# Where a recurrence's output products stand among the attention's scores, and which engine does one of the last additions

## The chip, the cores and the metric

The kernel runs on one core of one Trainium2 chip. The core has a matrix engine (TensorE, PE in the profile), a vector engine (VectorE, DVE), a scalar engine (ScalarE, ACT), a general engine (GpSimd, POOL) and SyncE (SP), which here only issues transfers. Each engine runs its own instructions in order, and they wait for one another by semaphores. The metric is the device time of one execution in microseconds (us). Of the kernel before the change three runs were timed: 451.43, 451.46 and 453.24 us, median 451.46. One further execution was profiled; all rows below are from it.

## The reference

One decoder layer on 512 tokens with 1024 features, in float32. Cut to what matters here:

```python
xn = rmsnorm(h)
aq, ak, av, ag, bq, bf, bi, bg, gate_a, gate_b = split(xn @ w_in)
ya = moba_attention(norm(aq), norm(ak), av)          # 8 heads x 64, relative-position bias
ya = (ya * silu(ag)) @ w_up_a
yb = hgrn2_chunkwise(silu(bq), kb, bi, log_f)        # 4 heads, state 128 x 128
yb = (rmsnorm(yb) * silu(bg)) @ w_up_b
merged = sigmoid(gate_a) * ya + sigmoid(gate_b) * yb
h = h + merged @ w_out
return h + (p @ w_ple) * sigmoid(h @ w_ple_gate)
```

Inside the recurrence, each chunk's output is `scores @ v + (q * exp(cum)) @ state`.

## The kernel before, in words

A large product is computed as three products of rounded halves (high x high, low x high, high x low; `mm3`, line 289), each weight and each operand being split into two float32r tiles by ScalarE (the high half) and VectorE (the rest). A projection of the 1024 features is 24 such products of 128 x 128 by 128 x 512. TensorE's order is written out by hand. A planner walks through the projections in the list `ORDER` and keeps a clock of its own (`now`): after every three products it adds their time and runs the side streams that are due (`tick`, `run_due`). A side stream is a generator that issues a piece of work and then names a delay or a condition for its next piece. The engines other than TensorE are not written out: a scheduler orders their instructions from dependences, priorities and a timing model, so that a small move on TensorE can turn over the order of VectorE, ScalarE and SP around it.

Two side streams matter.

The attention (`attention`, line 788) takes the eight heads as four head pairs (0 to 3) and each pair in two runs (`STEPS`): the first run has the query blocks 0, 1 and 2, the second has query block 3. A run issues its `scores` products (line 815), then `softmax`: VectorE subtracts from the bias and takes the row minimum (line 832), ScalarE takes the exponential and scales (834, 836), VectorE turns 32 x 32 blocks (839); then sixteen small transfers on SP's queue finish the transpose (line 850). The values follow at the end of a pair (`out_values`, line 863, tiles o0 to o3), behind the first scores of the next pair. `PACE` is the planner's delay between the runs: 19.5 behind a first run and 22.5 behind a second. Each pair needs two rows of bias, 256 KB each, which `bias` (line 880) loads on SP's queue into a pool of three buffers, 8 planner microseconds ahead of the pair's first run.

The recurrence (`hgrn_intra`, `hgrn_out`) goes through its four heads. For head h it prepares decayed keys and queries (the hx tiles), waits until an attention run has been issued (`beside_attention`, line 501), and computes small products for the scores inside a chunk (lpb, lpa: lines 592 to 649). `hgrn_out` computes the states (line 663, tiles hds and st). Its output products (tile hop, lines 678 and 680) are, for heads 0 to 2, not issued but put on the list `hops`; `hgrn_intra` of the next head takes them from there (line 583) behind its `beside_attention`, that is right behind the scores of an attention run, and ahead of its own lpb products. The output products add 1.5 to the planner's clock. The fourth head issues its own, without the list. Behind them ScalarE squares (692), VectorE applies gain and gate (695) and a norm follows (313 to 334, 698).

At the end of the kernel the last product is made in half sums for pairs of 128 output features. `merge` (line 1181) then takes the sigmoid, multiplies by the embedding's product (line 1189, VectorE), adds the residual (line 1190: VectorE for n = 3 and n = 7, otherwise GpSimd) and stores (line 1191, SP). The last pieces are output block n = 3: its right half, then columns 0 to 127 (product tile pe3l) and last columns 128 to 255 (pe3m).

Of the kernel before, what the change touches and what calls it, by code (L numbers as in the profile page):

```python
# [15 lines left out]
OP = mybir.AluOpType  # L16
# [12 lines left out]
LEVELS = (16, 8, 4, 2, 1)  # L29

STEPS = ((0, 1, 2), (3,))
PACE = (19.5, 22.5)

HP = 2.5
H0 = 8.0
# [33 lines left out]
def hybrid_layer_kernel(  # L69
# [17 lines left out]
    V, A, G, PE = nc.vector, nc.scalar, nc.gpsimd, nc.tensor  # L87
# [14 lines left out]
    def bank(tag, name):  # L102
        return psum.tile([128, 512], F32, tag=tag, bufs={"mm": 3, "g": 2, "a": 3}[tag], name=name)
# [34 lines left out]
    def cost(us):  # L138
        now[0] += us
# [18 lines left out]
    def held_from(us, insts, until=None):  # L158

        def later():  # L160
            for inst in insts if until not in done else []:
                held(inst)
            yield 0.0

        spawn(later(), us)
# [331 lines left out]
    hops = []  # L497
# [290 lines left out]
    def attention(qn, kn, va, sags, res):  # L788
        def place(qb, j):

            return {0: (j, 0), 1: (2, 256 * j), 2: (j, 128), 3: (j, 0)}[qb]

        def tiles(step):
            return 2 + (len(STEPS[step]) > 1)
# [3 lines left out]
        def scores(hp, step):  # L798
            (qh, ql), (kh, kl) = qn[hp], kn[hp]
            nt = tiles(step)  # L800

            sps = [bank("a", f"s{hp}{step}{i}") for i in range(nt)]
            extra = bank("mm", f"s{hp}{step}x") if nt > 2 else None

            def where(qb, j):
                b_, o = place(qb, j)
                return (extra, 0) if (qb, j) == (1, 1) else (sps[b_], o)

            for qb in STEPS[step]:
                nk = 128 * (qb + 1)  # L810
                for i in range(3):
                    for j in range(2):
                        js = slice(64 * j, 64 * j + 64)
                        b_, o = where(qb, j)
                        PE.matmul(b_[:, o:o + nk], (qh, ql, qh)[i][js, qb * 128:qb * 128 + 128], (kh, kh, kl)[i][js, :nk],
                                  start=(i == 0), stop=(i == 2))
            cost(sum(3 * max(0.107, (qb + 1) * 0.0538) for qb in STEPS[step]))
            return where

        def softmax(hp, step, T, where):  # L820

            nt = tiles(step)
            z = pb[:, Z0[step]:Z0[step] + nt].rearrange("p t f -> p (t f)").rearrange("p (b t f) -> p b t f", b=4, t=nt)
            with tc.high_priority(offset=AHEAD):
                left = [sum(place(qb, j)[0] == b for qb in STEPS[step] for j in range(2)) for b in range(nt)]
                for qb, j in [(qb, j) for qb in STEPS[step] for j in range(2)]:
                    b_, o = place(qb, j)
                    nk = 128 * (qb + 1)
                    p_ = pb[:, b_, o:o + nk]
                    st = unit("ps", f"ps{hp}{qb}{j}", shape=(128, 4))  # L830
                    s_, so = where(qb, j)
                    in_order(V.tensor_tensor_reduce(p_, s_[:, so:so + nk], T[j][:, nk - 1::-1], -1.0, 3e38,  # L832
                                                    OP.add, OP.min, st[:, 0:1]))
                    A.activation(p_, p_, AF.Exp, bias=st[:, 0:1], scale=-1.0, accum_out=st[:, 1:2])  # L834
                    V.reciprocal(st[:, 2:3], st[:, 1:2])
                    A.activation(p_, p_, AF.Copy, scale=st[:, 2:3])  # L836
                    left[b_] -= 1
                    if left[b_] == 0:
                        V.transpose(z[:, :, b_, :].rearrange("p b (n c) -> p b n c", c=32),  # L839
                                    pb[:, b_].rearrange("p (n b c) -> p b n c", b=4, c=32))  # L840
            return z

        def sorted_groups(step, z):

            nt = tiles(step)
            pt = pb[:, PT0[step]:PT0[step] + nt].rearrange("p t f -> p (t f)").rearrange("p (a t f) -> p a t f", a=4, t=nt)
            with tc.high_priority(offset=AHEAD):
                for a in range(4):
                    for b in range(4):
                        nc.sync.dma_start(pt[32 * b:32 * b + 32, a], z[32 * a:32 * a + 32, b])  # L850
            return pt.rearrange("p a t (n c) -> p a (t n) c", c=32)

        def out_values(hp, pts):

            o = bank("mm", f"o{hp}")
            for step, pt in enumerate(pts):
                for qb in STEPS[step]:
                    qs = slice(qb * 128, qb * 128 + 128)
                    for kb in range(qb + 1):
                        for j in range(2):  # L860
                            h0 = hp * 128 + 64 * j
                            b_, o0 = place(qb, j)
                            PE.matmul(o[64 * j:64 * j + 64, qs], va[kb][:, h0:h0 + 64], pt[:, :, 4 * b_ + o0 // 128 + kb, :],
                                      start=(kb == 0), stop=(kb == qb))
            cost(1.5)
            sag = sags[hp]
            V.tensor_tensor(sag, o, sag, op=OP.mult)
            h_ = unit("A", f"yah{hp}", R)
            l_ = unit("A", f"yal{hp}", R)
            split(h_, l_, sag)  # L870
            res.append((h_, l_))
            done.add(f"ya{hp}")
# [3 lines left out]
        def bias(hp):  # L876
            for j in range(2):
                t = unit("T", f"bias{hp}{j}")
                row = ed[2 * hp + j:2 * hp + j + 1, :]
                held(nc.sync.dma_start(t, bass.AP(tensor=row.tensor, offset=row.offset, ap=[[1, 128], [1, 512]])))  # L880
                T[hp, j] = t
# [10 lines left out]
        for n in range(len(steps) + 1):  # L892
            ahead = BIAS if 0 < n < len(steps) and steps[n][1] == 0 else 0.0
            if n >= 1:
                yield PACE[steps[n - 1][1]] - ahead
            if ahead:
                bias(steps[n][0])
                yield ahead
            if n < len(steps):
                hp, i = steps[n]  # L900
                where = scores(hp, i)
            if n >= 1 and steps[n - 1][1] == NS - 1:
                ho = steps[n - 1][0]
                while f"ag{ho}" not in done:
                    yield lambda: f"ag{ho}" in done
                out_values(ho, [pts.pop(n - NS + i_) for i_ in range(NS)])
            if n < len(steps):
                z = softmax(hp, i, [T[hp, 0], T[hp, 1]], where)
                if others:
                    parts.clear()  # L910
                    others.pop()()
                    for n_, p_ in enumerate(list(parts)):
                        held_from(16.0 + 2.0 * n_, [p_])
                pts[n] = sorted_groups(i, z)
            runs[0] += 1
# [124 lines left out]
    hf, xt, wt, edge = {}, {}, {}, []  # L1040
# [140 lines left out]
    def merge(n, c, ps, pes, t, plus=None):  # L1181
        if plus is not None:
            with tc.high_priority(offset=AHEAD):
                V.tensor_tensor(t[:, c], ps, plus, op=OP.add)  # L1184
            ps = t[:, c]
        if ps is not None:
            A.activation(t[:, c], ps, AF.Sigmoid)  # L1187
        yield
        V.tensor_tensor(t[:, c], t[:, c], pes()[:, c], op=OP.mult)
        (V if n % 4 == 3 else G).tensor_tensor(t[:, c], t[:, c], hf[n][:, c], op=OP.add)  # L1190
        nc.sync.dma_start(out[n][:, c], t[:, c])

    for p in range(4):
# [29 lines left out]
        for step in order:  # L1223
            if step == "E0":
                ple(pe0, n0, whole)
            elif step == "E1":
                ple(pe1, n1, whole)
            elif step == "E0r":
                ple(pe0, n0, rh)
            elif step == "E0l":  # L1230
                pe2 = bank("mm", f"pe{n0}l")
                ple(pe2, n0, slice(0, 128))
                ends[2] = merge(n0, slice(0, 128), None, lambda: pe2, t0)
                pe4 = bank("a", f"pe{n0}m")
                ple(pe4, n0, slice(128, 256))
                ends["last"] = merge(n0, slice(128, 256), None, lambda: pe4, t0)
                for e in (2, "last"):
                    next(ends[e])
            else:
                product(step)  # L1240
# [105 lines left out]
```

## Time and profile before

| | us |
|---|---|
| median of the three timed runs | 451.46 |
| the profiled execution's own time | 452.42 |
| its span from the first to the last instruction | 450.6 |
| TensorE busy | 445.8 |
| VectorE busy | 334.6 |
| ScalarE busy | 289.7 |
| GpSimd busy | 59.9 |

A row of the order of time reads: start, duration, engine, line of the kernel, operation, out<-in, shape, count, and in brackets how long the engine had stood idle and what ended that. Rows of one line that follow each other are merged. TensorE's products are pipelined: a row's duration is longer than the distance to the next start, and it is the distance that counts. The granted clock of TensorE was 0.999 over the span. SPq and POOLq are the queues on which SP and GpSimd issue transfers.

### The profile page before, as it was taken

To read this page: it belongs to the slowest core of one execution; us is meant where nothing else is said; L and a number is where in the kernel's file an instruction comes from. 1 tells how busy PE (TensorE), PEld (TensorE's weight loads), DVE (VectorE), ACT (ScalarE), POOL (GpSimd) and SP (SyncE) were. 2 spreads that over 40 slices of the span, in tenths; PEclk is the share of its full clock that TensorE was granted. 3 is DMA by queue.
4 is the path that set the end of the run, shared out by engine and by line. 5 is a ranking of instruction groups with operands and counts; after the bars stand their busy time and mean duration, and the time that the engine had idled before them with its cause. 6 is when DMAs were issued, how large, how long until landed. Compare 5 with 4: busy or idle time off the path is not lost.

```text
span 450.6 us, 8536 instructions
## 1 busy us (share of the span) xinstructions
PE 445.8 (99%) x3192; PEld 376.2 (83%) x3192; DVE 334.6 (74%) x682; ACT 289.7 (64%) x561; POOL 59.9 (13%) x97
## 2 busy tenths in 40 slices
PE   9999999999999999999999999999999999999996
PEld 8888888888878888878887888878888888899996
DVE  5869494776899797949857775465479868999844
ACT  5958474746689988979857996784135434555421
POOL 1000100000000101010100000111210103325520
PEclk9999999999999999999999999999999999999999
DMA  8802424168594455171425444265551444312111
GB/s 265 317 1 94 141 93 129 48 219 197 167 215 127 159 134 178 46 203 49 142 93 155 140 135 148 70 197 149 184 173 47 168 145 143 129 47 95 49 47 48
DMA packets 32857, 59.53 MB, mean 132 GB/s; under 512 B 7088, under 2 KB 18736, under 8 KB 32816
## 3 DMA queue, kind: packets, MB, share of 16 engines
q0 software_dynamic: 9056, 32.51, 22.5%
q1 hardware_dynamic: 23616, 26.47, 20.4%
q8 instruction: 25, 0.41, 0.4%
q14 instruction: 16, 0.13, 0.1%
q10 hardware_dynamic: 144, 0.01, 0.0%
HBM read 48.74 MB, written 4.98 MB: 119 GB/s over the span
## 4 chain that ended last, share of the span: by engine, by line
PE 89%; DVE 5%; SPq 2%; DMA 1%; issue 1%; ACT 0%; DVEq 0%
PE h L293 10%; PE g L1210 9%; PE ga L293 9%; PE gb L293 7%; PE ub L293 5%; PE aq L423 5%; PE ak L423 5%; PE ua L293 5%; PE av L423 5%; PE bf L293 5%; PE bi L423 5%; PE bq L293 4%; PE bg L293 4%; PE ag L293 4%; PE pe L293 2%; SPq L850 2%
## 5 line engine op out<-in xcount | busy, mean ns | idle before, releaser
L276 ACT ACTIVATE wh<-wf 128x1024 fp32r<-128x1024 f32 (+1 forms) x70 | 67.0, 958 | 63.2 <-issue 9.8
L277 DVE TENSOR_TENSOR wl<-wf,wh 128x1024 fp32r<-128x1024 f32 (+1 forms) x70 | 76.8, 1097 | 38.0 <-ACT wh L276 35.7
L266 POOL DMA_DIRECT2D wf<-in_w_tr_dram x30 | 15.8, 528 | 170.5 <-DVE wl L277 115.4
L293 PE MATMUL ga<-xh,wh 128*128 128x512 f32 x64 | 25.3, 396 | 0.4 <-DVE bg3s L491 0.4
L293 PE MATMUL gb<-xh,wh 128*128 128x512 f32 x64 | 25.0, 391 | 0.0
L293 PE MATMUL ga<-xh,wl 128*128 128x512 f32 x64 | 24.9, 390 | 0.0
L293 PE MATMUL ga<-xl,wh 128*128 128x512 f32 x64 | 24.9, 389 | 0.0
L293 PE MATMUL gb<-xl,wh 128*128 128x512 f32 x64 | 24.9, 389 | 0.0
L293 PE MATMUL h<-mh,wh 128*128 128x512 f32 x64 | 24.9, 389 | 0.0
L293 PE MATMUL h<-ml,wh 128*128 128x512 f32 x64 | 24.9, 389 | 0.0
L293 PE MATMUL h<-mh,wl 128*128 128x512 f32 x64 | 24.9, 389 | 0.0
L293 PE MATMUL gb<-xh,wl 128*128 128x512 f32 x64 | 24.9, 389 | 0.0
L834 ACT ACTIVATE pb<-pb,ps 128x128 f32<-128x128 f32 (+3 forms) x32 | 17.6, 551 | 10.0 <-DVE ps L832 10.0
L832 DVE CUSTOM_DVE_ANT_0 pb<-s,bias 128x128 f32<-128x128 f32 (+3 forms) x28 | 12.8, 493 | 7.1 <-DMA bias<-in_ed_dram 4.8
L1187 ACT ACTIVATE sg<-sg 128x256 f32<-128x256 f32 x12 | 5.0, 414 | 20.2 <-DVE sg L1184 20.2
L836 ACT ACTIVATE pb<-pb,ps 128x128 f32<-128x128 f32 (+3 forms) x32 | 16.0, 550 | 0.0
L542 ACT ACTIVATE hx<-hx 128x512 f32<-128x512 f32 x24 | 14.9, 623 | 1.4 <-DVE hx L541 1.3
L266 POOL DMA_DIRECT2D wf<-in_w_up_dram x16 | 8.6, 538 | 52.2 <-DVE wl L277 32.2
L839 DVE STREAM_TRANSPOSE pb<-pb 128x512 f32<-128x512 f32 x20 | 13.8, 696 | 2.0 <-ACT pb L836 2.0
L266 POOL DMA_DIRECT2D wf<-in_w_tok_dram x8 | 4.4, 549 | 80.2 <-DVE wl L277 68.2
L293 PEld LDWEIGHTS ga<-xh,wh 128*128 128x128 f32 x64 | 12.0, 188 | 3.5 <-DVE bg3s L491 0.8
L293 PEld LDWEIGHTS ga<-xh,wl 128*128 128x128 f32 x64 | 12.0, 188 | 2.6
(958 smaller groups left out, 1434.9 us busy)
## 6 DMA issues: line engine op xcount, KB each, us to landing
wf<-in_w_tr_dram POOLq DMA_DIRECT2D x30, 512.0 KB, 4.2
wf<-in_w_tok_dram POOLq DMA_DIRECT2D x8, 512.0 KB, 3.6
wf<-in_w_up_dram POOLq DMA_DIRECT2D x16, 256.0 KB, 3.0
wf<-in_w_o_dram POOLq DMA_DIRECT2D x8, 512.0 KB, 3.8
wf<-in_w_g_dram POOLq DMA_DIRECT2D x8, 512.0 KB, 3.6
wf<-in_w_tok_dram SPq DMA_DIRECT2D x6, 512.0 KB, 7.6
pb<-pb SPq DMA_DIRECT2D x64, 48.0 KB, 2.9
bias<-in_ed_dram SPq DMA_DIRECT2D x8, 256.0 KB, 4.1
```

The source lines that it names most:

```text
L266: (G if len(wraw) >= FAR else nc.sync).dma_start(raw, ap)
L276: rounds[i] = A.activation(hi, wraw[i], AF.Copy)
L277: V.tensor_tensor(lo, wraw[i], hi.bitcast(F32), op=OP.subtract)
L293: dense.append(PE.matmul(ps, a[:, k, :], b[k], start=(n == 0), stop=(n == tot - 1)))
L423: dense.append(PE.matmul(banks[t], a[:, s_], b[:, kk, :], start=(k == 0 and i == 0), stop=(k == KD - 1 and i == 2)))
L542: A.activation(x, x, AF.Exp)
L832: in_order(V.tensor_tensor_reduce(p_, s_[:, so:so + nk], T[j][:, nk - 1::-1], -1.0, 3e38, OP.add, OP.min, st[:, 0:1]))
L834: A.activation(p_, p_, AF.Exp, bias=st[:, 0:1], scale=-1.0, accum_out=st[:, 1:2])
L836: A.activation(p_, p_, AF.Copy, scale=st[:, 2:3])
L839: V.transpose(z[:, :, b_, :].rearrange("p b (n c) -> p b n c", c=32), pb[:, b_].rearrange("p (n b c) -> p b n c", b=4, c=32))
L850: nc.sync.dma_start(pt[32 * b:32 * b + 32, a], z[32 * a:32 * a + 32, b])
L1210: dense.append(PE.matmul(dst[i], a[:, k], b, start=(m == 0 and i in (1, 6, 5)), stop=(m == 11), skip_group_check=i not in (1, 6, 5)))
```

## The change

Three edits. The delay behind a second run is 21.0 for 22.5. Ahead of the scores of a second run (`i` is the run, 0 or 1) the attention takes the output products that wait in the list and issues them, so that `hgrn_intra` finds the list empty. And the addition for columns 0 to 127 of output block 3 goes to GpSimd.

```diff
-PACE = (19.5, 22.5)
+PACE = (19.5, 21.0)
...
             if n < len(steps):
                 hp, i = steps[n]
+                while i and hops:
+                    hops.pop()()
                 where = scores(hp, i)
...
         V.tensor_tensor(t[:, c], t[:, c], pes()[:, c], op=OP.mult)
-        (V if n % 4 == 3 else G).tensor_tensor(t[:, c], t[:, c], hf[n][:, c], op=OP.add)
+        (V if n % 4 == 3 and c != slice(0, 128) else G).tensor_tensor(t[:, c], t[:, c], hf[n][:, c], op=OP.add)
         nc.sync.dma_start(out[n][:, c], t[:, c])
```

Line numbers behind line 900 are two higher in the changed kernel. In the rows below the number behind a name counts buffers and differs between the two kernels.

TensorE, at the second run of head pair 1, before (bq is the projection that is under way, s the scores, hop the output products of head 1):

```order
L293 MATMUL bq_2219<-xh_412,wl_2139 128x512
L815 MATMUL s_2223<-kh_1131,qh_878 128x512
L815 MATMUL s_2224<-kh_1131,qh_878 128x512
L815 MATMUL s_2223<-kh_1131,ql_882 128x512
L815 MATMUL s_2224<-kh_1131,ql_882 128x512
L815 MATMUL s_2223<-kl_1135,qh_878 128x512
L815 MATMUL s_2224<-kl_1135,qh_878 128x512
L678 MATMUL hop_2259<-sc,biv_393 128x128 x2
```

And the same place in the changed kernel:

```order
L293 MATMUL bq_2219<-xh_412,wl_2139 128x512
L678 MATMUL hop_2223<-sc,biv_393 128x128 x2
L680 MATMUL hop_2223<-ha_1320,st_2072 128x128
L678 MATMUL hop_2223<-sc,biv_396 128x128
L680 MATMUL hop_2223<-ha_1320,st_2072 128x128
L678 MATMUL hop_2223<-sc,biv_396 128x128
L680 MATMUL hop_2223<-ha_1320,st_2072 128x128
L815 MATMUL s_2231<-kh_1131,qh_878 128x512
```

Six scores products and the output products have changed places; in both kernels the lpb products (line 592) come next. The same holds in pairs 0 and 2, and nothing else moves on TensorE but o3, which stands nine projection products earlier.

SP's queue between the first and the second run of pair 1 (hkt2there is the recurrence's key transpose, pb the attention's, the bias rows are those of pair 2):

```order
 L627 DMA hkt_2390<-hkt2there 32x4x96
-L850 DMA pb<-pb 32x256 x16
 L880 DMA bias_2497<-in_ed_dram 128x512
 L880 DMA bias_2499<-in_ed_dram 128x512
+L850 DMA pb<-pb 32x256 x16
```

The two bias loads have passed the sixteen transfers. In pairs 0 and 2 SP's order is as before.

VectorE ahead of the second transpose of pair 1's second run, in the kernel before (hx are the recurrence's tiles, npart and nms belong to the norm behind the output products, hu is a scan for the next head):

```order
L839 STREAM_TRANSPOSE pb<-pb 128x4x128
L571 COPY_PREDICATED s_2097<-mkf,lpb_2267 128x64
L543 TENSOR_TENSOR hx_2_2485<-hk_1789,hx_2_2485 128x128x2
L548 TENSOR_TENSOR hx_2_2485<-ha_1780,hx_2_2485 128x128x2
L523 SCALAR_TENSOR_TENSOR hu_2411<-onec,ha_2407 128x128 x4
L277 TENSOR_TENSOR wl_2431<-wf_2428,wh_2430 128x1024
L320 TENSOR_REDUCE nms<-nquad 32x16
```

And in the changed kernel:

```order
L571 COPY_PREDICATED s_2097<-mkf,lpb_2296 128x64
L519 TENSOR_TENSOR ha_2407<-ha_2407,hu_2411 128x512
L320 TENSOR_REDUCE nms<-nquad 32x16
L543 TENSOR_TENSOR hx_2_2485<-hk_1789,hx_2_2485 128x128x2
L548 TENSOR_TENSOR hx_2_2485<-ha_1780,hx_2_2485 128x128x2
L839 STREAM_TRANSPOSE pb<-pb 128x4x128
L523 SCALAR_TENSOR_TENSOR hu_2411<-onec,ha_2407 128x128 x4
```

The transpose now follows lines 571, 320, 543 and 548, which it preceded (519 preceded it before as well). Farther ahead, line 695 and line 313 of the output products have moved from behind the run's bias operations into the midst of them.

## The prediction

> **What bounds the kernel now.** I read the page's head first, then the list of all of TensorE's waits.
>
> ```profile
> span 450.6 us, 8536 instructions
> PE   445.8 (99%) x3192; PEld 376.2 (83%) x3192; DVE 334.6 (74%) x682; ACT 289.7 (64%) x561; POOL 59.9 (13%) x97
> ...
> PE warm L193 <- PEq L1334: 0.8, 1, 0.8
> PE ga L293 <- DVE bg3s L491: 0.4, 1, 0.4
> ```
>
> TensorE is busy for 445.8 of 450.6 us. The 4.8 us that are left are all named: 0.8 at the start, one wait of 0.4 for VectorE, and 3.6 behind the last product, which ends at 447.00 (its row is in term 4). So the time is the sum of TensorE's products, and the change keeps every one of them. It can only take away the 0.4, fill or open small gaps between products, open a new wait, or change the 3.6 at the end. Waits of other engines, however long, are outside the sum until one reaches TensorE.
>
> I set the sum against the profiled execution: 452.42 us, which is its span and 1.82 around it. The median of the three timed runs is 451.46, so 0.96 less; I carry differences from one to the other unchanged.
>
> **The one wait, and what makes it late.** TensorE around it, with the releaser in brackets:
>
> ```profile
> 242.34 0.39 PE L293 MATMUL ga<-xl,wh 128*128 128x512 f32 x1
> 242.57 0.39 PE L293 MATMUL ga<-xh,wl 128*128 128x512 f32 x1
> 243.36 0.50 PE L293 MATMUL ga<-xh,wh 128*128 128x512 f32 x1 [0.40 <-DVE bg3s L491]
> 243.69 0.39 PE L293 MATMUL ga<-xl,wh 128*128 128x512 f32 x1
> ```
>
> The usual distance from start to start is 0.23 (242.34 to 242.57). Across the wait it is 0.79, and the next one is 0.33. The wait therefore costs (0.79 - 0.23) + (0.33 - 0.23) = 0.66 us, not 0.40. The product needs the bank that bg3s still occupies, and line 491 frees it about that much too late. Following VectorE back, its backlog starts where the two bias rows of head pair 2 arrive late:
>
> ```profile
> 212.99 10.98 SPq L850 DMA_DIRECT2D pb<-pb  x16
> 224.01 1.06 SPq L880 DMA_DIRECT2D bias<-in_ed_dram  x2
> ...
> 202.53 0.68 DVE L832 CUSTOM_DVE_ANT_0 pb<-s,bias 128x512 f32<-128x512 f32 x1
> ...
> 228.31 0.29 DVE L832 CUSTOM_DVE_ANT_0 pb<-s,bias 128x128 f32<-128x128 f32 x1 [3.24 <-DMA bias<-in_ed_dram]
> 230.21 0.29 DVE L832 CUSTOM_DVE_ANT_0 pb<-s,bias 128x128 f32<-128x128 f32 x1 [1.60 <-DMA bias<-in_ed_dram]
> ...
> 227.12 2.40 PE L863 MATMUL o<-pb,avv 128*64 128x128 f32 x40
> ```
>
> On SP's queue the two bias loads (line 880) stand behind the sixteen transfers of line 850, and VectorE stands idle for 3.24 and then 1.60 us until they land, although the scores are there before 227.12, where the next products begin.
>
> **Term 1: the bias loads of pair 2 move ahead of the sixteen transfers.** The rows of SP's queue above show it. The first load's buffer was last read in pair 0, so it need not wait; the second waits for the last reader of its buffer, the line 832 that ran at 202.53. In the new order that one starts near 203.8 (scores end 1.2 us later, below). Both are issued by about 205 and, with the worst landing of bias loads before, 228.31 - 224.01 = 4.3 and 230.21 - 224.64 = about 5.6, are there by 211. So the chain for pair 2 starts at about 227.1 instead of in two pieces from 228.31 and 230.21; its end comes about 2.9 us earlier, and line 491 with it. It was less than 0.7 late, so the wait goes: **-0.66 us** (bounds -0.67 and 0). What is late next on VectorE is unimportant, as no other product waits in the whole span.
>
> **Term 2: products before scores (three places).** The same products in another order differ only in what it costs TensorE to go from one kind to the next:
>
> ```profile
> 200.77 0.39 PE L293 MATMUL bq<-xh,wl 128*128 128x512 f32 x1
> 201.09 0.50 PE L815 MATMUL s<-kh,qh 64*128 64x512 f32 x2
> ...
> 201.66 0.40 PE L815 MATMUL s<-kl,qh 64*128 64x512 f32 x2
> 201.99 0.71 PE L678 MATMUL hop<-sc,biv 128*128 128x128 f32 x4
> 203.74 0.43 PE L592 MATMUL lpb<-hx 128*32 128x64 f32 x16
> ...
> 290.48 0.39 PE L293 MATMUL ga<-xh,wl 128*128 128x512 f32 x1
> 290.71 0.60 PE L678 MATMUL hop<-sc,biv 128*128 128x128 f32 x4
> ```
>
> From a projection into the scores it is 0.32 (200.77 to 201.09), 0.09 above the usual 0.23; from the scores into the output products 0.33, 0.10 above. The fourth head shows the way that is new: from a projection straight into the output products it is 0.23, with nothing on top. The steps from products into scores, and from scores into lpb, are in no row. I take each as equal to the one it replaces and so save 0.09 at each of three places: **-0.3 us**. Bounds: if the other steps cost nothing either -0.6, if they cost 0.2 each more than now +0.3.
>
> The products move ahead by the scores' 0.9 us (201.09 to 201.99). Their inputs come last for head 2, whose products stood at 251.29, and for the fourth head, whose products stay at 290.71:
>
> ```profile
> 242.39 1.25 ACT L654 ACTIVATE sc<-s 32x128 f32<-32x128 f32 x4
> ...
> 285.07 0.30 DVE L670 SCALAR_TENSOR_TENSOR st<-st,hu,hds 128x128 f32<-128x128 f32 x1
> ```
>
> The first is over at 243.64, so 7.6 us are left, and 6.7 after the move: no new wait.
>
> **Term 3: what the delayed scores push back.** The scores end 203.74 - 201.99 less 0.1, so some 1.65 us later, and VectorE's first line 832 of the pair, at 202.53 before, starts about 1.2 later. Behind it, lines 571, 320, 543 and 548 now precede the second transpose, about 0.9 together. The transpose feeds the sixteen transfers and these feed the second half of the products o1:
>
> ```profile
> 212.26 0.70 DVE L839 STREAM_TRANSPOSE pb<-pb 128x512 f32<-128x512 f32 x1
> ...
> 222.43 1.54 SPq L850 DMA_DIRECT2D pb<-pb  x1
> ...
> pb<-pb SPq DMA_DIRECT2D x1, 32.0 KB, 2.8
> ...
> 259.78 10.01 SPq L850 DMA_DIRECT2D pb<-pb  x16
> 276.42 2.40 PE L863 MATMUL o<-pb,avv 128*64 128x128 f32 x40
> ...
> 305.83 10.03 SPq L850 DMA_DIRECT2D pb<-pb  x16
> 323.45 2.40 PE L863 MATMUL o<-pb,avv 128*64 128x128 f32 x40
> ```
>
> The last transfer was issued at 222.43 and landed 2.8 later, at 225.2. The o products start at 227.12; the first 24 of 40 records use the first run's values, so the second half is due at 227.12 + 24/40 x 2.40 = 228.6. That is 3.4 of cover. I put the shift at 1.2 + 0.9 = 2.1: **0 us**. Past 3.4 each further microsecond would be TensorE's. For pair 0 the new order puts only line 320 (about 0.2) in front. For pair 2 I count about 3.3, but o2 starts at 276.42 and its transfers were issued by 269.8, which leaves over 5. There the two bias loads of pair 3 stay behind the sixteen transfers and come 3.3 later, so VectorE begins pair 3 up to 2 us late; the fourth head's products at 290.71 had their last state by 285.4, so that is covered as well.
>
> The smaller pace (21.0 for 22.5) is used up in pairs 0 to 2 by the products' 1.5, which are now counted ahead of it: no row of TensorE moves there except the swap. In pair 3, with no products to count, o3 moves nine projection products ahead, about 2 us. Its transfers were issued by 315.9, the products stood at 323.45: **0 us**.
>
> **Term 4: the end.** The last VectorE operations, TensorE's last product, SP's last issue, and what GpSimd took for this addition at twice the width:
>
> ```profile
> 446.72 0.28 PE L293 MATMUL pe3m<-ph,pwl 128*128 128x128 f32 x1
> 446.43 0.29 DVE L1189 TENSOR_TENSOR sg<-sg,pe3l 128x128 f32<-128x128 f32 x1 [0.28 <-PE pe3l L293]
> 446.75 0.29 DVE L1190 TENSOR_TENSOR sg<-sg,hf 128x128 f32<-128x128 f32 x1
> 447.04 0.29 DVE L1189 TENSOR_TENSOR sg<-sg,pe3m 128x128 f32<-128x128 f32 x1
> 447.36 0.29 DVE L1190 TENSOR_TENSOR sg<-sg,hf 128x128 f32<-128x128 f32 x1
> ...
> 447.68 0.33 SPq L1191 DMA_DIRECT2D out_dram<-sg  x1
> ...
> 435.74 0.41 DVE L1189 TENSOR_TENSOR sg<-sg,pe 128x256 f32<-128x256 f32 x1
> 436.24 0.73 POOL L1190 TENSOR_TENSOR sg<-sg,hf 128x256 f32<-128x256 f32 x1 [1.97 <-DVE sg L1189]
> ...
> 404.52 1.22 DVE L1052 TENSOR_TENSOR w21l<-pb,w21h 128x1024 fp32r<-128x1024 f32 x1
> 405.05 1.29 POOL L1190 TENSOR_TENSOR sg<-sg,hf 128x256 f32<-128x256 f32 x1
> ```
>
> Taking away the addition at 446.75 frees 0.29 on VectorE, but the multiplication behind it needs the product that ends at 447.00, and it started at 447.04 already: at most 0.04 is won. GpSimd starts 0.09 behind a multiplication (436.15 to 436.24), so at 446.81. Its 128x128 addition is in no row: at most the 0.73 of twice the width, at least VectorE's 0.29; I take 0.5. It ends at 447.31, SP issues at about 447.35 and is free at 447.68, just when the second half is due: **0 us**. With 0.73 the second issue slips to about 447.92, +0.24.
>
> The Trainium skill, in "GPSIMD Engine Reference", section "Elementwise — side-by-side cycle accounting", puts a two-input addition on GpSimd at 1.96 times VectorE's; 1.96 x 0.29 would be an estimate of 0.57, and the end about 0.07 later than by my 0.5.
>
> **Sum.** 452.42 - 0.66 - 0.3 + 0 + 0 = 451.46 for a profiled execution; less 0.96 this is **450.5 us** for the median, 0.2% below 451.46. A measurement of this kernel tells about 0.5%, 2.3 us, from no change.
>
> **The rivals.**
> *The wait only moves (0.15).* Line 491 also follows three ScalarE operations that could be late for another reason, or the gain of the steps between products is not there. Then only one of the two terms comes, or neither: 450.8 to 451.5. For it: ScalarE has no idle time in that stretch. Against it: ScalarE itself had waited for the late bias.
>
> *GpSimd and VectorE block each other at the end (0.12).* The addition at 405.05 took 1.29 for 0.73, while a VectorE subtraction with both inputs in SBUF ran until 405.74. At the end VectorE's last addition, also from SBUF alone, is due at 447.36. If GpSimd is still at work, VectorE's addition waits: with 0.73 it starts at 447.54, the end is +0.2; with 1.29 at 448.1, +0.75. With the other terms: 450.7 to 451.3. The Trainium skill states this rule in "SBUF — State Buffer", section "Who interferes with whom": of a VectorE instruction with two SBUF inputs and a GpSimd instruction that reads SBUF, the later one is blocked until the other is done. By that rule, and the row at 405.05 agrees, this half of the change can only cost.
>
> *The second half of o1 comes late: slower (0.07).* Place: 228.6. If lines 832 to 839 of pair 1 slip not 2.1 but 6 us, because every step between ScalarE and VectorE waits anew, TensorE stands for 6 - 3.4 = 2.6 us: 450.5 + 2.6 = 453.1. It decides from 3.4 on; from 4.4 on the change is slower than 451.46. Against it speaks that both engines were nearly unbroken in work there, so operations that change places cost little.
>
> *The change does nothing (0.06):* neither term, 451.46.
>
> **How the numbers follow.** My forecast has 0.60: 450.2 to 450.8. For the range I add the bounds: all gains at their ends, 450.5 - 0.3 - 0.04, and 0.2 for the repetitions, gives 450.0; above it takes in no gain (451.5) and half of the o1 rival: 452.2. Faster by over 0.5% would need 449.2, and no term reaches that: 0.03. Slower by over 0.5%, above 453.7, needs a slip of more than 6.6 us: 0.04. The same: 0.93.
>
> **What would show it.** In the profile after: no wait of TensorE but the first; the two bias loads issued before the sixteen transfers of pair 1; the first line 832 of pair 2 at about 227 with no wait for a DMA; 0.23 from the last projection product into each hop; SP's last issue 0.9 to 1.1 behind the start of TensorE's last product, as in 446.72 to 447.68. I am wrong if TensorE waits at o1 or at a hop, or if GpSimd's addition takes over 0.6.

## The result, and the profile after

| | before | after |
|---|---|---|
| median of six timed runs each | 451.82 us | 455.9 us |
| the profiled execution's own time | 452.42 us | 455.63 us |
| its span | 450.6 us | 453.9 us |
| start of TensorE's last product | 446.72 us | 446.26 us |

The changed kernel is slower: ratio 1.0091, 95% interval 1.0070 to 1.0112. The range on record ended at 452.2. Yet TensorE did not get slower. The first two rows are of the page of the changed kernel, the two below of the list of all of TensorE's waits:

```profile
span 453.9 us, 8535 instructions
...
PE 445.4 (98%) x3192; PEld 376.4 (83%) x3192; DVE 334.4 (74%) x681; ACT 289.8 (64%) x561; POOL 60.7 (13%) x98
...
PE warm L193 <- PEq L1336: 0.8, 1, 0.8
PE o L863 <- DMA pb<-pb: 0.3, 2, 0.2
```

Busy time is 0.4 lower, the wait at ga is gone, two small ones at o have come. The last product starts 0.46 earlier than before. So the loss lies behind the last product. Nor is it the clock: the granted clock averages 0.995 over the span, for 0.999 before, but it is 1.00 in the changed kernel up to 449.0 and 0.50 only behind that, where TensorE has nothing left to do. The end of the changed kernel in order of time (start, duration, engine, line):

```profile
445.71 1.97 SPq L1193 DMA_DIRECT2D out_dram<-sg  x3
446.26 0.28 PE L293 MATMUL pe3m<-ph,pwl 128*128 128x128 f32 x1
446.39 0.46 POOL L1192 TENSOR_TENSOR sg<-sg,hf 128x128 f32<-128x128 f32 x1 [9.88 <-DVE sg L1191]
446.57 0.29 DVE L1191 TENSOR_TENSOR sg<-sg,pe3m 128x128 f32<-128x128 f32 x1 [0.32 <-PE pe3m L293]
446.89 0.29 DVE L1192 TENSOR_TENSOR sg<-sg,hf 128x128 f32<-128x128 f32 x1
```

Everything is computed by 447.18 and the last store is issued by 445.71 + 1.97 = 447.68, which was 448.01 before (447.68 + 0.33); still the span goes to 453.9. What remains are instructions of the queues, which no count of busy time contains. They stand under the kernel's last line (1343, in the kernel before 1341); the columns are the count, the shortest, median and longest duration in ns, and the first and the last start. First the changed kernel:

```profile
L1343 POOLq EVENT_SEMAPHORE  x4: 17/17/17, 452.7 to 453.8; - x4
L1343 POOLq DRAIN  x3: 40/241/6289, 446.4 to 453.6; - x3
L1343 SPq DRAIN  x3: 7/7/7, 449.2 to 452.9; - x3
```

Then the kernel before:

```profile
L1341 SPq DRAIN  x3: 7/7/7, 449.5 to 449.8; - x3
L1341 POOLq EVENT_SEMAPHORE  x4: 17/17/17, 449.6 to 450.5; - x4
L1341 POOLq DRAIN  x3: 40/93/6577, 436.2 to 450.1; - x3
```

At the end a DRAIN stands on the queue of every engine, then event semaphores, by which the engines wait for one another. SP's comes when its last store has landed: 449.5 before, 449.2 after. GpSimd's first DRAIN starts with its last addition and lasts 6577 ns before (436.2 + 6.6 = 442.8, long over when SP comes) and 6289 ns after (446.4 + 6.3 = 452.7). GpSimd's first semaphore follows at once: 449.6 before, right behind SP, and 452.7 after, right behind its own DRAIN. The end has moved from SP to GpSimd, by 452.7 - 449.2 = 3.5 us.

The DRAIN is far longer than the addition it stands behind. Without the addition's 0.46 it is 6.29 - 0.46 = 5.83; before, 6.58 - 0.73 = 5.85. So the change cost nothing by the addition's own time. It moved a closing piece of 5.8 us from 437.0 to 446.9.

### The profile page after: what moved, and what is told of

Read it like the earlier page. It is cut to its first block, busy times and chain, and to the rows that moved or that the text cites. A ratio compares the mean times of both kernels' runs of the same rounds, so it can differ in the third digit from the quotient of the medians.

```text
span 453.9 us, 8535 instructions
## 1 busy us (share of the span) xinstructions
PE 445.4 (98%) x3192; PEld 376.4 (83%) x3192; DVE 334.4 (74%) x681; ACT 289.8 (64%) x561; POOL 60.7 (13%) x98
## 3 DMA queue, kind: packets, MB, share of 16 engines
q0 software_dynamic: 9056, 32.51, 21.0%
## 4 chain that ended last, share of the span: by engine, by line
PE 87%; SPq 4%; DVE 3%; ACT 2%; DMA 1%; issue 1%; DVEq 0%
PE ga L293 10%; PE h L293 10%; PE g L1212 9%; PE gb L293 5%; PE ub L293 5%; PE aq L423 5%; PE ag L293 5%; PE ak L423 5%; PE ua L293 5%; PE av L423 5%; PE bf L293 5%; PE bi L423 5%; SPq L850 4%; PE bg L293 3%; PE bq L293 3%; PE pe L293 2%
```

## The experiments

The theory after the result: GpSimd's DRAIN takes about 5.8 us behind its last operation, whatever that is, and it sets the end as soon as it is over later than SP's last store. The rival: the swap on TensorE and the smaller pace made the rest late, and the addition is a bystander. Each run stands beside runs of the kernel before on the same chip (median 452.48 us for e1 to e4, 452.77 for e5 to e8, a single run of 451.92 for e9 and e10, and 452.17 for e11).

### The change in two parts

The changed kernel with the old addition, and the kernel before with the new one:

```diff
# e1_no_gpsimd, against the changed kernel
-        (V if n % 4 == 3 and c != slice(0, 128) else G).tensor_tensor(
+        (V if n % 4 == 3 else G).tensor_tensor(
# e2_gpsimd_only, against the kernel before
-        (V if n % 4 == 3 else G).tensor_tensor(
+        (V if n % 4 == 3 and c != slice(0, 128) else G).tensor_tensor(
```

> The changed kernel with the GpSimd edit undone (swap and pace stay). Theory D (GpSimd's closing drain, about 5.8 us behind its last operation, ends the program): GpSimd's last operation is again the one at about 436, its drain is over at about 442, so the end is no longer its; TensorE's last product starts near 446.26 as in the changed kernel, span 450.1 to 450.3, time 0.4 to 0.5 below before. Rival R (the longer end comes with the swap and the pace, not with GpSimd): span stays at about 453.9, time about 3.5 above before.

> Before with only the addition moved to GpSimd. Theory D: the addition ends at about 447.3, the drain at 453.1, span 454.2, time about 3.6 above before, a little more than the whole change, since TensorE gains nothing. Rival S (the addition costs only its own time and the block between the two engines): at most 0.75 above before, span up to 451.3. Rival R: no difference.

Measured: without the addition on GpSimd 452.67 us, ratio 1.0001 (0.9981 to 1.0021); with nothing but it 456.5 us, ratio 1.0090 (1.0070 to 1.0110). The whole loss comes with the addition, and with the other two edits none that could be told from zero (0.2% either way). The rival is out. The gain of 0.4 to 0.5 that e1 was expected to show does not show either.

### How late, and how much

Three kernels set the place and the size of GpSimd's last operation apart from each other. e3 gives GpSimd an addition of one column behind the store of block 3's right half, whose result nobody reads (it is work on top of the kernel's). e4 and e5 give it the first or the second half of block 7, of 256 columns (in order of time: the right half comes first). All three are the kernel before otherwise:

```diff
# e3_one_column_late
         nc.sync.dma_start(out[n][:, c], t[:, c])
+        if n == 3 and c == slice(256, 512):
+            z = sb.tile([128, 1], F32, tag="z", bufs=1, name="z")
+            G.tensor_tensor(z, t[:, 256:257], hf[n][:, 256:257], op=OP.add)
# e4_first_half_of_7 (e5_second_half_of_7: slice(0, 256) for slice(256, 512))
-        (V if n % 4 == 3 else G).tensor_tensor(
+        (V if n % 4 == 3 and not (n == 7 and c == slice(256, 512)) else G).tensor_tensor(
```

> Before plus one GpSimd addition of a single column (128x1, into a tile that nobody reads) behind VectorE's addition at 445.73 to 446.15. No other engine's order changes and nothing waits for it. Theory D: it ends at about 446.4, drain until 452.2, span about 453.2, time 2.6 above before, although it is hardly any work. Rival S: nothing waits for it, so 0. A drain that grows with the work of the last operation: well below 1.

> Before with the first addition of block 7 (VectorE at 441.24, 128x256) moved to GpSimd instead. Theory D: it ends at about 442.0, drain over at 447.9, before the last store has landed (about 449.5): span 450.6, no difference to before within 0.2. If any late addition on GpSimd were dear for another reason (a block of VectorE, SP's queue), about the same 3 us as the whole change.

> Before with the second addition of block 7 (VectorE at 444.70, 128x256) moved to GpSimd. Theory D: GpSimd from about 444.3 to 445.0, drain over at about 450.85, 1.2 behind the point (449.6) at which SP is ready, so span about 451.8 and time 1.2 above before: a third of the whole change's loss for an addition 2.2 us earlier. Rival (a fixed cost of a late GpSimd operation): 0 or the whole 3.3.

The closing DRAINs, as above. In e3, whose GpSimd operation is line 1194:

```profile
L1344 POOLq DRAIN  x3: 93/188/6034, 445.7 to 452.5; - x3
L1344 SPq DRAIN  x3: 7/7/7, 449.0 to 452.0; - x3
```

In e4, with the first half of block 7:

```profile
L1341 POOLq DRAIN  x3: 40/241/6571, 440.1 to 449.2; - x3
L1341 SPq DRAIN  x3: 7/7/7, 448.3 to 448.6; - x3
```

In e5, with the second half:

```profile
L1341 POOLq DRAIN  x3: 40/241/6577, 445.0 to 452.6; - x3
L1341 SPq DRAIN  x3: 7/7/7, 450.2 to 451.9; - x3
```

| | GpSimd's last operation starts, us | its shape | its duration, us | length of the DRAIN less this, us | DRAIN over at, us |
|---|---|---|---|---|---|
| before | 436.24 | 128x256 | 0.73 | 5.85 | 442.8 |
| e4 | 440.11 | 128x256 | 0.74 | 5.83 | 446.7 |
| e5 | 445.07 | 128x256 | 0.74 | 5.84 | 451.6 |
| e3 | 445.74 | 128x1 | 0.19 | 5.84 | 451.7 |
| after | 446.39 | 128x128 | 0.46 | 5.83 | 452.7 |

Behind the operation the DRAIN takes the same, whether that has 1, 128 or 256 columns. In e4 it is over 1.6 ahead of SP, so it is hidden: 452.54 us, ratio 0.9995 (0.9978 to 1.0012). In e5 it is over 1.4 behind SP: 454.24 us, ratio 1.0027 (1.0013 to 1.0042), which is 1.2 us as expected. In e3 it is 2.7 behind SP: 455.11 us, ratio 1.0063 (1.0040 to 1.0086), 2.9 us. An addition of a single column, off every path of data, costs 0.6% by its place alone.

### What the DRAIN pays for

In this kernel GpSimd also issues the weight loads behind the tenth. The list of DMA issues of the changed kernel, with KB of each and the median us from issue to landing, has 70 of them:

```profile
wf<-in_w_tr_dram POOLq DMA_DIRECT2D x30, 512.0 KB, 3.9
wf<-in_w_tok_dram POOLq DMA_DIRECT2D x8, 512.0 KB, 3.6
wf<-in_w_up_dram POOLq DMA_DIRECT2D x16, 256.0 KB, 2.9
wf<-in_w_o_dram POOLq DMA_DIRECT2D x8, 512.0 KB, 4.8
wf<-in_w_g_dram POOLq DMA_DIRECT2D x8, 512.0 KB, 3.4
```

The last is issued at 404.0 and lands 3.4 later, so all have landed long before the end. Three kernels, each the changed one otherwise, give none, one or the first 35 of them to GpSimd and the others to ScalarE's queue:

```diff
-            (G if len(wraw) >= FAR else nc.sync).dma_start(raw, ap)
# e7_no_gpsimd_dma
+            (nc.scalar if len(wraw) >= FAR else nc.sync).dma_start(raw, ap)
# e9_one_gpsimd_dma
+            (G if len(wraw) == FAR else nc.scalar if len(wraw) > FAR else nc.sync).dma_start(raw, ap)
# e10_half_gpsimd_dma
+            (G if FAR <= len(wraw) < FAR + 35 else nc.scalar if len(wraw) >= FAR else nc.sync).dma_start(raw, ap)
```

> The changed kernel with all weight loads issued by ScalarE's queue instead of GpSimd's, so that GpSimd issues no transfer at all. Only the drain's length is asked for, not the time, which will differ as ScalarE is then held up. If the 5.8 us are spent on the transfers that GpSimd had issued: the drain is under 1 us behind its last addition, as its first one of the program (0.19). If they belong to any drain behind GpSimd's arithmetic: again 5.8.

> The changed kernel, but of the weight loads behind the tenth only the first is issued by GpSimd (about 48 us into the run, 512 KB, landed some 400 us before the end), the others by ScalarE. Theory A: the drain behind GpSimd's last operation costs a fixed amount as soon as GpSimd has issued any transfer: drain 6.0 to 6.4 us, span about 6.3 us behind the end of GpSimd's last addition. Theory B: the drain's length goes with the number of transfers issued (69 or 70 give 5.83, so about 0.08 each): drain 0.6 to 0.7 us including the 0.46 of the addition, span as in e7_no_gpsimd_dma (about 451.5). The other loads on ScalarE cost about what they did there.

> As the run before, with the first 35 of the 70 loads on GpSimd, the last of them some 200 us before the end. Theory A (fixed as soon as there is one): drain 6.0 to 6.4 us. Theory B (goes with the number): 0.46 + 35/70 of 5.83 = about 3.4 us. A third: the drain is long only where a GpSimd transfer is recent: drain about 0.55 us here and in the run before.

GpSimd's closing DRAINs with no transfer on GpSimd:

```profile
L1343 POOLq DRAIN  x3: 34/77/548, 447.9 to 451.3; - x3
```

With one:

```profile
L1343 POOLq DRAIN  x3: 40/89/645, 447.1 to 450.5; - x3
```

With 35:

```profile
L1343 POOLq DRAIN  x3: 40/102/3431, 446.9 to 450.9; - x3
```

The last addition took 0.46, 0.45 and 0.45 us in them.

| transfers issued by GpSimd | DRAIN without the addition, us | less the 0.09 of none, for each |
|---|---|---|
| 0 (e7) | 0.548 - 0.46 = 0.09 | |
| 1 (e9) | 0.645 - 0.45 = 0.20 | 0.11 |
| 35 (e10) | 3.431 - 0.45 = 2.98 | 0.083 |
| 70 (after) | 6.289 - 0.46 = 5.83 | 0.082 |

The DRAIN goes with the number of transfers: 0.08 us each, although all of them are long done. It does not go with their bytes: 35 of 512 KB against 54 of 512 and 16 of 256 KB would give 0.09 + 2.89 x 62/35 = 5.2, not 5.83. Nor does it go with the packets of GpSimd's transfers (5040 in e10, 9056 in the changed kernel): 0.09 + 2.89 x 9056/5040 = 5.3. With 35 transfers the DRAIN is still the last thing at the end, over at 450.3 when SP's comes at 449.5. The spans are 451.5, 450.8 and 451.1; each of the three kernels has one run only (453.62, 452.68 and 452.9 us, against 452.77, 451.92 and 451.92 before), too few to compare their times.

The last run uses this. The first of GpSimd's three closing DRAINs alone is long, the other two take 40 and 241 ns. If a DRAIN settles the transfers once, another one may do it earlier, in the 9.88 us in which GpSimd waits for its last addition:

```diff
# e11_early_drain, against the changed kernel, in part (plus_h: the addition of line 1192;
# added: a list, empty at first; behind(a, b): the scheduler keeps a behind b)
+        if n % 4 < 3:
+            added.append(plus_h)
+        if n == 3 and c == slice(256, 512):
+            added.append(behind(G.drain(), added[-1]))
+        if n == 3 and c == slice(0, 128):
+            behind(plus_h, added[-1])
```

> The changed kernel with one DRAIN more: on GpSimd, right behind its last addition but one (the sg of output block 2, ends about 436.5 us), where GpSimd then stands idle for 9.9 us. Nothing else moves on any engine. Theory A (the drain pays about 0.08 us for each of the 70 transfers that GpSimd has issued since the last drain, once): the added drain takes about 5.8 us and ends about 442.4, before the last addition is due at 446.4; the closing drain is then 0.5 to 0.6 us including the 0.46 of the addition, its barrier is ready before SyncE's (about 449.2), the span is 449.9 to 450.3, and the time is that of before: ratio 0.996 to 1.001. Theory B (the closing drain costs 5.8 whatever came before it, or the transfers' bookkeeping is not ended by a drain in the middle): closing drain 6.3 us, ratio 1.009 as in the changed kernel.

The new DRAIN (line 1198) and the closing ones (line 1351):

```profile
L1198 POOLq DRAIN  x1: 6581/6581/6581, 435.7 to 435.7; - x1
...
L1351 POOLq EVENT_SEMAPHORE  x4: 17/17/17, 449.2 to 450.2; - x4
L1351 POOLq DRAIN  x3: 34/154/541, 446.3 to 450.0; - x3
L1351 SPq DRAIN  x3: 7/7/7, 449.1 to 449.7; - x3
```

The early DRAIN starts with the last addition but one (435.71, 0.74 long), takes the 6.58 us and is over at 442.3; the last addition starts at 446.33, unhindered, and the closing DRAIN takes 0.54, as with no transfers at all. SP is last again (449.1, then GpSimd's semaphore at 449.2). 453.0 us beside 452.17, ratio 1.0008 (0.9992 to 1.0025). One instruction takes the whole loss away, and the addition stays on GpSimd.

### The swap and the pace alone

e6 is the swap with the old pace and the old addition; e8 is the kernel before with the new pace:

```diff
# e6_swap_old_pace, against e1
-PACE = (19.5, 21.0)
+PACE = (19.5, 22.5)
# e8_pace_only, against the kernel before
-PACE = (19.5, 22.5)
+PACE = (19.5, 21.0)
```

> The swap without the GpSimd edit and with the old pace 22.5. The o products then stand about 1.5 us later behind their transfers in pairs 0 to 2, so the waits of o0 and o1 (0.42 and 0.37 in the changed kernel) go. If these waits are what kept TensorE's gain at 0.46: TensorE's last product about 0.8 earlier than in e1, span about 449.4, time about 1.2 below before. If the waits only move with the scheduler's new order: as e1, 0.4 below before.

> Before with only the pace 21.0. The o products come 1.5 us earlier than before in pairs 0 to 2 while their transfers do not: o0 was covered by about 1.0 and would wait about 0.5; the bias rows of pair 2 stay behind the sixteen transfers as before and are needed 1.5 earlier, so the wait of 0.66 at the ga product stays or grows. Time 0 to 2 above before; the swap and not the pace carries the gain. Rival: the pace alone gives the gain of 0.46.

Measured: 452.85 us, ratio 1.0006 (0.9986 to 1.0026), and 452.24 us, ratio 0.9990 (0.9972 to 1.0008). Neither can be told from the kernel before, nor from e1. The gain expected of e6 does not show in its time. Its last product starts at 445.63 in the profile, against 445.85 in e1 and 446.17 in e8; but where no edit has moved anything yet, the first product of the bf projection starts between 48.08 (e4) and 49.23 (e5), so single executions differ by more than the gain sought. Counted from a product at about 145, ahead of every move, the last product comes about 0.8 sooner than in the kernel before in e6, but also about 0.4 sooner in e4, whose order on TensorE is the old one. The expectation for e8 was wrong in its mechanism: the transfers of pair 1 started at 207.55 for 212.99, not at their old time, and its profile has neither a wait at o nor the one at ga.

No version here beats the kernel before by more than its interval: e1, e4, e6, e8 and e11 are all even with it.

## Why the prediction was wrong

**Term 4, the end, is the step that failed: it put the end at 0, and the runs showed +3.5.** It followed the addition's result, to SP's store, and got that right: GpSimd's addition took 0.46 where 0.5 was taken, and SP's queue was done 0.33 earlier than before. But it took the stretch behind the last product, 3.6 us before, as something that only a late store could lengthen. It did not ask what else the end waits for on the queue that was given new work: that other engines' waits are outside the sum until one reaches TensorE does not hold behind TensorE's last product. The rows of line 1341 would have told it: GpSimd's DRAIN ended 5.85 behind its last operation, and the barrier began at 449.6. With Term 4's own end of the addition, 447.31 + 5.85 = 453.16, 3.56 behind that; the sum would have been 451.46 + 3.56 = 455.02 for the profiled execution, which took 455.63. What the length comes from, 70 transfers at 0.08, no row of before shows; the length itself was there to be read.

The bounds failed with it: +0.24 and +0.75 were the prices of a slower addition, not of a later one.

**Term 1, the bias loads: the path was right, the size holds for some executions only.** Pair 2's first bias operation starts at 227.23, forecast 227.1, and waits for a product, no longer for a load:

```profile
227.23 0.29 DVE L832 CUSTOM_DVE_ANT_0 pb<-s,bias 128x128 f32<-128x128 f32 x1 [1.86 <-PE s L815]
```

Line 491 runs at 240.0, where it ran at 242.6, and TensorE's wait for bg3s is in no profile with the swap. Its size was less firm than 0.66: with the products in their old place that wait was 0.4 in the kernel before and in e2, 0.3 in e3, 0.8 in e5, and it is absent in e4 and e8. It goes with the bias loads, as Term 1 has it: line 832 of pair 2 stands 3.9 to 4.9 us for them in the four profiles that have the wait, and not at all in e4 and e8. So the swap gains this only in an execution in which the loads would have come too late.

**Term 2, products before scores: right, and more than forecast.** TensorE at the second run of pair 1, in the changed kernel (hop's first and last rows, the scores, the next kind, the next projection):

```profile
200.92 0.39 PE L293 MATMUL bq<-xh,wl 128*128 128x512 f32 x1
201.15 0.60 PE L678 MATMUL hop<-sc,biv 128*128 128x128 f32 x4
...
202.80 0.50 PE L815 MATMUL s<-kh,qh 64*128 64x512 f32 x2
203.13 0.39 PE L815 MATMUL s<-kh,ql 64*128 64x512 f32 x2
203.36 0.40 PE L815 MATMUL s<-kl,qh 64*128 64x512 f32 x2
203.69 0.43 PE L592 MATMUL lpb<-hx 128*32 128x64 f32 x16
...
205.05 0.50 PE L293 MATMUL bq<-xh,wh 128*128 128x512 f32 x1
```

And where the same projection goes on in the kernel before:

```profile
205.10 0.50 PE L293 MATMUL bq<-xh,wh 128*128 128x512 f32 x1
```

From a projection into the products it is 0.23, as said. Projection to projection it is 4.13 (200.92 to 205.05), and was 4.33 (200.77 to 205.10): 0.20 saved. The step into the products gave the 0.09 of the forecast; the rest comes within the first four output products, which take 0.44 to the next row (201.15 to 201.59) for 0.54 (201.99 to 202.53). In pairs 0 and 2 it is 0.08 and 0.21 by the same rows, 0.5 together for the forecast 0.3.

**Term 3, the delayed scores: the shift was right, the cover was not.** Pair 1's transfers started 2.2 us later, forecast 2.1, but TensorE waited. SP's queue and the products o1, changed kernel:

```profile
215.19 10.88 SPq L850 DMA_DIRECT2D pb<-pb  x16
...
225.48 0.59 SPq L850 DMA_DIRECT2D pb<-pb  x1
...
pb<-pb SPq DMA_DIRECT2D x1, 32.0 KB, 3.2
...
227.13 1.53 PE L863 MATMUL o<-pb,avv 128*64 128x128 f32 x24
228.81 1.09 PE L863 MATMUL o<-pb,avv 128*64 128x128 f32 x16 [0.15 <-DMA pb<-pb]
229.83 1.03 PE L563 MATMUL lpa<-hx 128*32 128x16 f32 x96
```

The last transfer was issued at 225.48, where it was 222.43, and took 3.2 to land for 2.8: there at 228.7 for 225.2, 3.5 later, when the cover was 3.4. Its own issue had been long before (1.54) and was short now (0.59), so it started 3.05 later though the queue ended only 2.1 later. From their start to lpa the products take 229.83 - 227.13 = 2.70, for 2.33 before (227.12 to 229.45): 0.37. That is the mechanism of the rival "the second half of o1 comes late", at its threshold. In pair 0 the prediction had counted a shift of 0.2 and no cover, and the wait is of the same size (2.75 for 2.33): the cover there was only about 1.0, the last transfer was there at 179.9 for 178.9, and the products themselves started 0.26 earlier. The two together eat most of Term 2's gain. In e6, with the old pace, TensorE has no wait at o.

**The sum.** On TensorE -0.66, -0.5 and +0.8 give about -0.4, and the last product started 0.46 earlier. That the two agree is in part luck. Up to the last projection product ahead of the first swap TensorE runs the same products in the same order. That product in the kernel before:

```profile
152.17 0.39 PE L293 MATMUL bf<-xh,wl 128*128 128x512 f32 x1
```

And in the changed kernel:

```profile
151.94 0.39 PE L293 MATMUL bf<-xh,wl 128*128 128x512 f32 x1
```

So 0.23 of the lead was there already, and 0.23 is what TensorE won behind this. At the end: +3.5 for 0. By the timed runs the change costs 455.9 - 451.82 = 4.1, interval 3.2 to 5.1.

**The rivals.** "GpSimd and VectorE block each other" was not tested: GpSimd was done at 446.85, 0.04 ahead of VectorE's addition. By the Trainium skill's figure ("GPSIMD Engine Reference", section "Elementwise — side-by-side cycle accounting") the estimate for the addition was 0.57; the trace has 0.46 beside VectorE's 0.29, so 1.6 times at this size. The rival that lost the time was not on the list: all of them asked when the result is there, none asked when GpSimd is done. The 0.04 for slower was too small for a change that gives an engine new work in the last microsecond.

## What to carry to other kernels

Work given to another engine near the end moves the end of that engine's queue too: look up in the profile's rows of the last line when each engine's closing DRAIN ends, and compare with the one that comes last. On GpSimd that DRAIN took 0.08 us for every transfer that it had issued since its last DRAIN, so its last operation belongs that much ahead of the end, or an earlier DRAIN into one of its pauses. For a queue of transfers, cover is counted to the landing of the last one in each version, not from the shift of the first.

## What the runs showed of the hardware that was not expected

GpSimd's DRAIN pays for transfers that landed long ago: 0.09 us with none issued, 0.20 with one, 2.98 with 35, 5.83 with 70, independent of the operation ahead of it (1, 128 or 256 columns) and paid only once (0.54 with the addition in the closing DRAIN behind an early one). SP's DRAINs take 7 ns, though line 850 alone has 128 transfers on its queue. What GpSimd does in these 0.08 us for each transfer no run shows.
